# S5's outputs by pairs of octets, and b's gates as two units of seven block products behind w_proj_b

## The chip, the cores and the metric

One core of a Trainium2 chip runs the whole kernel as one launch. The metric is the device time of one execution in microseconds (us), taken as the median over runs. Five engines work side by side, each through its own queue in order: TensorE (PE) multiplies, VectorE (DVE) and ScalarE (ACT) work on elements, GpSimd (POOL) does small things and starts DMAs that add onto their target, and SyncE (SP) starts the plain DMAs.

## The reference, cut to what matters

One encoder layer over 512 tokens of width 1024, in float32. Two mixers run side by side on the normed input n and are merged by gates:

```python
n = rms_norm(h, mix_norm_g[i])
proj = n @ w_in[i]
xa, zu, zv = proj[..., :OFF_U], proj[..., OFF_U:OFF_V], proj[..., OFF_V:OFF_GA]
gate_a = jax.nn.sigmoid(proj[..., OFF_GA:OFF_GB])
gate_b = jax.nn.sigmoid(proj[..., OFF_GB:])
ya = s5_branch(xa, ...)   # two scans, gelu, then y * sigmoid(y @ w_glu)
yb = sgu_branch(zu, zv, ...)
merged = gate_a * (ya @ w_proj_a[i]) + gate_b * (yb @ w_proj_b[i])
h = h + merged @ w_out[i]
h = h + memory_cross_attention(...)
h = h + swiglu(rms_norm(h, ffn_norm_g[i]), w_gate[i], w_up[i], w_down[i])
```

The change touches gate_b, `yb @ w_proj_b` and the end of s5_branch. Each is 1024 wide, but for S5, which is 512 wide: 32 groups of 16 channels with 64 complex states a group.

## The kernel before

**Precision.** Every matrix product takes float32 operands split into a high half (ACT casts, line 85) and a low half (DVE subtracts, line 86) by `split`, and sums three matmuls: high x high, high x low, low x high.

**Weights.** `plan` is a list of weight blocks in the order in which the products use them. `next_w` hands out the next one; on the way it starts the loads of later blocks (each load has its own lead, 3 entries in most cases) and splits blocks up to two entries ahead. Raw blocks, high halves and low halves have three buffers each, so a block can be split when the product three before it is done. `plan_feat` plans blocks of 512 rows and 256 columns. `plan_sums` hangs other transfers on plan entries: sums of blocks of w_q and w_down that are built in DRAM (a plain copy on SP, and some entries later an addition on POOL), for use much later.

**Products.** `feat` computes two groups of 128 output features over all 512 tokens: 2 x 4 x 3 matmuls of 512 columns for a block. `product` (line 1370) is used further on, for the queries and the feed-forward part: there a matrix product is split in 2 x 2 blocks, and seven block products of 256 columns, with sums of blocks taken before and after, stand for eight. The numbers 1 to 7 name them. In the feed-forward units GpSimd and DVE build the sums of the weight blocks (lines 175 to 184).

**Order.** After the projection zu (`zu_evac`, lines 1144 to 1145) makes yb_hi and yb_lo in the slots E and D, the gates of b and w_proj_b alternate by column groups of 256: sigmoid on ACT into `part` (slot A, line 1155), then `pb_evac` multiplies `part` by w_proj_b's result on DVE (line 1158). Then come w_glu and w_proj_a. A scheduler at compile time orders the instructions of each engine, by program order among those that are ready; what is marked `in_order` keeps its order.

**S5 beside it.** `s5_program` is a generator that `tick` advances while the projections run, one unit of `side["now"]` for each 5.2 us of products; `later` calls a function some units on. For each octet of groups `s5_kernels` builds small kernels (through DRAM, kd to tt) and `s5_outputs` makes the outputs: the states are copied, shifted by one (`ss`, lines 952 and 953), `mix_` multiplies (line 966), gelu on ACT (line 972), four transposes (line 978), a copy, and eight stores into `yd` in DRAM, half of them from SP and half from ACT (line 986). The octets go 0, kernels 2, 1, kernels 3, 2, 3. Behind w_proj_b `finish_side` runs out what is left, S5's pool is closed, and a pool "merge" opens; `ygt` is loaded from yd (line 1174), split into yg, and read by w_glu.

**Tags.** Tiles of one tag share buffers: a new tile waits until all uses of the old one are done. `zh` holds S5's states, `u` its inputs, `e0`, `e1`, `tt`, `wt` and `etmp` its work tiles.

Of the kernel before, what the change touches and what calls it, by code (L numbers as in the profile page):

```python
# [9 lines left out]
F32 = mybir.dt.float32  # L10
# [7 lines left out]
P = 128  # L18
D = 1024
# [33 lines left out]
def hybrid_layer_kernel(  # L53
# [157 lines left out]
    def plan_queries():  # L211

        for q, n in ((1, 0), (5, 0), (2, 0), (6, 0), (1, 1), (7, 0), (2, 1), (4, 0), (3, 0),
# [7 lines left out]
            plan.append(((w_q, 512 * n, q), [(LOADS, load)], lambda got=got: halves(got.pop("raw"))))  # L221

    def plan_units(units, down):
# [86 lines left out]
    for i in range(4):  # L310
# [225 lines left out]
    s5 = ExitStack()  # L536
    s5p = s5.enter_context(tc.tile_pool(name="s5", bufs=1))


# [61 lines left out]
    ud = dp.tile([SW, Q, NCH], F32, name="ud")  # L601
    yd = [dp.tile([GO * C, Q, NCH], F32, name=f"yd{o}") for o in range(NO)]
    st = {}
# [25 lines left out]
    def s5_setup():  # L629
# [22 lines left out]
        raw_b = s5p.tile([P, 2, G, C], F32, tag="tt", name="raw_b", bufs=2)  # L652
        raw_c = s5p.tile([P, 2, G, C], F32, name="raw_c")
        brow = s5p.tile([2 * G, 2, 64, C], F32, tag="u", name="brow")
# [92 lines left out]
        yield 1.5  # L747
        zr = s5p.tile([P, G, C], F32, name="bbr")
        zi = s5p.tile([P, G, C], F32, name="bbi")
        w = s5p.tile([P, 2, G, C], F32, tag="etmp", name="bbw")  # L750
# [15 lines left out]
        for j in range(4):  # L766
            nc.sync.dma_start(dcol[32 * j:32 * j + C, :],
                                s5_d[0].rearrange("(q j c) -> j c q", j=4, c=C)[j])
        st["dmask"], st["dcol"] = dmask, dcol
        yield 0.3  # L770
# [170 lines left out]

    def s5_outputs(o):
        gs = slice(o * GO, (o + 1) * GO)
        while ("oct", o) not in st:
            yield None
        e_re, e_im, tt = st["oct", o]
        zh, u = st["zh"], st["u"]
        ss = s5p.tile([P, 2, GO, NCH], F32, tag="wt", name="ss", bufs=2)
        zv = zh[:, :, :, gs].rearrange("p n i g -> p i g n")
        nc.gpsimd.memset(ss[lo_, :, :, 0:1], 0.0)  # L950
        nc.gpsimd.memset(ss[hi_, :, :, NCH - 1:NCH], 0.0)
        nc.scalar.copy(ss[lo_, :, :, 1:NCH], zv[lo_, :, :, 0:NCH - 1])
        nc.scalar.copy(ss[hi_, :, :, 0:NCH - 1], zv[hi_, :, :, 0:NCH - 1][:, :, :, ::-1])
        ss = (ss[:, 0], ss[:, 1])

        yt = tt.rearrange("p (i r) c -> p i r c", i=2)

        def mix_():
            ps = aux("py", (P, GO // 2, P))
            for r in range(GO // 2):  # L960
                for k in range(3):
                    for j in range(2):
                        g = 2 * r + j
                        a = (u[:, o * GO + g, :], ss[0][:, g, :], ss[1][:, g, :])[k]
                        b = (tt[:, g, :], lc(e_re, g), lc(e_im, g))[k]
                        in_order(nc.tensor.matmul(ps[64 * j:64 * j + 64, r, :], a, b, start=r == k == 0, stop=k == 2,  # L966
                                                  tile_position=(0, 64 * j), skip_group_check=True))
            later(0.5, lambda: squash(ps))

        def squash(ps):  # L970

            nc.scalar.activation(yt[:, 0], ps, AF.Gelu_apprx_tanh)
            later(1, back)

        def back():
            ps = aux("pyt", (P, GO // 2, P))
            for r in range(GO // 2):
                nc.tensor.transpose(ps[:, r, :], yt[:, 0, r, :], ident)
            later(0.5, lambda: emit(ps))

        def emit(ps):
            nc.scalar.copy(yt[:, 1], ps)
            y = yt[:, 1].rearrange("p r (g n) -> p (r g) n", n=NCH)
            ydo = yd[o].rearrange("(g c) l n -> l c g n", c=C)
            for l in range(Q):
                (nc.sync, nc.scalar)[l % 2].dma_start(ydo[l], y[C * l:C * l + C])

        later(0.5, mix_)
        yield 0.1
        yield None  # L990

    def s5_program():
# [15 lines left out]
        for _ in range(2):  # L1008
            yield None
        for o in range(NO):  # L1010
            yield from s5_outputs(o)
            if o + 2 < NO:
                yield from s5_kernels(o + 2)

# [138 lines left out]

    def gb_evac(m, j, ps):
        nc.scalar.activation(part[:, m - OFF_GB // P, :], ps, AF.Sigmoid)

    def pb_evac(m, j, ps):
        nc.vector.tensor_tensor(part[:, m, :], ps, part[:, m, :], ALU.mult)

    for c0 in range(0, D, 256):  # L1160
        feat(w_in, OFF_GB + c0, xn, KD, gb_evac)
        feat(w_proj_b, c0, yb, KD, pb_evac)
    finish_side()
    s5.close()
    mgx = ExitStack()
    mgp = mgx.enter_context(tc.tile_pool(name="merge", bufs=1))
    align(mgp)


    yg_hi = mgp.tile([P, 4, T], F32R, name="yg_hi")  # L1170
    yg_lo = mgp.tile([P, 4, T], F32R, name="yg_lo")
    ygt = mgp.tile([P, 4, T], F32, name="ygt")
    for m in range(4):
        nc.sync.dma_start(ygt[:, m, :], yd[m].rearrange("p l n -> p (l n)"))
        split(yg_hi[:, m, :], yg_lo[:, m, :], ygt[:, m, :])
    ya_hi = mgp.tile([P, 4, T], F32R, name="ya_hi")
    ya_lo = mgp.tile([P, 4, T], F32R, name="ya_lo")

    def glu_evac(m, j, ps):
        z = np_.tile([P, T], F32, tag="ev", name="glu", bufs=2)  # L1180
        nc.scalar.activation(z, ps, AF.Sigmoid)
        z2 = np_.tile([P, NCH, Q], F32, tag="ev", name="glu2", bufs=2)
        nc.vector.tensor_tensor(z2.rearrange("p n l -> p l n"), z.rearrange("p (l n) -> p l n", l=Q),
                                ygt[:, m, :].rearrange("p (l n) -> p l n", l=Q), ALU.mult)
        split(ya_hi[:, m, :], ya_lo[:, m, :], z2.rearrange("p n l -> p (n l)"))

    for c0 in range(0, SW, 256):
        feat(w_glu, c0, (yg_hi, yg_lo), 4, glu_evac)

# [4 lines left out]
    for c in range(KD // 2):  # L1194
        gat[c] = mgp.tile([P, 2, T], F32, tag="gat", name="gat", bufs=3)
        nc.sync.dma_start(gat[c], gad[2 * c:2 * c + 2].rearrange("m p t -> p m t"))
# [7 lines left out]
    for c0 in range(0, D, 256):  # L1204
        feat(w_proj_a, c0, (ya_hi, ya_lo), 4, pa_evac)
    mgx.close()

# [76 lines left out]

    K0, K1, T0, T1 = slice(0, 4), slice(4, 8), slice(0, 256), slice(256, 512)
    hops = {q: (hn_hi[:, ks, ts], hn_lo[:, ks, ts])
# [73 lines left out]

    def product(ps, u, q, start, ops):

        hi, lo = next_w(u[0], u[1], q)
        for j in range(2):
            cs = slice(j * P, (j + 1) * P)
            for k in range(4):
                a = (hi[:, k, cs], lo[:, k, cs])
                b = (ops[q][0][:, k, :], ops[q][1][:, k, :])
                for i, (x, y) in enumerate(((0, 0), (0, 1), (1, 0))):
                    nc.tensor.matmul(ps[:, j, :], a[x], b[y], start=start and j == k == i == 0,  # L1370
                                     stop=k == 3 and i == 2, skip_group_check=True)
        tick(2.7)

    def unit_bank(name):
        return bank(name).rearrange("p (j t) -> p j t", j=2)
# [9 lines left out]
    def kept(x, name):  # L1385
        t = np_.tile([P, 2, 256], F32, tag="ev", name=name, bufs=2)
        nc.scalar.copy(t, x)
        return t

    def minus(x, t):  # L1390
        nc.vector.tensor_tensor(t, x, t, ALU.subtract)
        return t


# [380 lines left out]
```

## Time and profile before

| | us |
|---|---|
| runs | 877.23 median of 3 (876.22 to 877.63) |
| the profiled execution | 877.18 |
| its span, first to last instruction | 875.4 |

In the page, busy time is given for each engine as a share of the span; the chain that ended last is the path that is followed back from the last instruction. In the chain in order of time and in a timeline each row has its start, its length, the engine, the line of the kernel and what was written from what. A matmul's row is longer than the distance to the next, as matmuls overlap in the array; the pace is the distance of starts.

### The profile page before, as it was taken

Reading aid. Unit: us, or ns where it says so; the run is one execution under the profiler, and the core shown is the slowest. Engines: PE = TensorE matmul, PEld = TensorE weight load, DVE = VectorE, ACT = ScalarE, POOL = GpSimd, SP = SyncE. Lnnn points to the kernel's source line nnn. Section 1 sums busy time; section 2 is a strip of 40 time slices with the busy share of each in tenths; the row PEclk is TensorE's granted clock in tenths of the full one; section 3 lists DMA queues with packets and bytes.
Section 4 is the critical chain, followed back from the end, with each engine's and each line's share of the span. In section 5 each row is a group of like instructions: output and inputs, shape, how many; then the busy total and the mean of one; then the engine's idle time right before and its main releaser. Section 6 shows DMA issues by size and latency. Waiting matters only on the chain.

```text
span 875.4 us, 14560 instructions
## 1 busy us (share of the span) xinstructions
PE 862.9 (99%) x5753; PEld 759.9 (87%) x5753; DVE 617.4 (71%) x867; ACT 464.1 (53%) x684; POOL 104.9 (12%) x154
## 2 busy tenths in 40 slices
PE   9999999999999999999999999999999999999996
PEld 6787888887888888889899878999999999888875
DVE  5699679968313258669657646767877768898875
ACT  5544875277434234557557444645545454556663
POOL 1001065103311100110000001001111110000000
PEclk9999999999999999999999999999999999999998
DMA  8358369943759946825687144547788963256672
GB/s 260 112 148 249 78 200 257 248 125 107 205 133 278 263 134 211 270 88 174 196 262 218 52 137 128 145 129 187 178 217 212 233 165 79 82 166 198 194 249 87
DMA packets 112134, 154.34 MB, mean 176 GB/s; under 512 B 13545, under 2 KB 78593, under 8 KB 112002
## 3 DMA queue, kind: packets, MB, share of 16 engines
q1 hardware_dynamic: 93042, 128.27, 45.2%
q0 software_dynamic: 16432, 24.09, 16.6%
q10 hardware_dynamic: 2592, 1.05, 0.5%
q8 instruction: 45, 0.74, 0.3%
q14 instruction: 23, 0.19, 0.1%
HBM read 146.60 MB, written 38.24 MB: 211 GB/s over the span
## 4 chain that ended last, share of the span: by engine, by line
PE 93%; DVE 5%; ACT 1%; issue 1%; POOL 0%; POOLq 0%
PE pf L350 29%; PE pt L350 17%; PE px L1370 12%; PE dx L350 7%; PE pq L1370 6%; PE dq L350 3%; PE pv L1370 3%; PE qx L1370 2%; PE dv L350 2%; PE ptr L511 1%; PE py L966 1%; PE po L350 1%; PE qq L1370 1%; DVE wlo L86 1%; PE pz L902 1%; PE pw L883 1%
## 5 line engine op out<-in xcount | busy, mean ns | idle before, releaser
L86 DVE TENSOR_TENSOR wlo<-wraw,whi 128x1024 fp32r<-128x1024 f32 (+1 forms) x139 | 165.0, 1187 | 110.2 <-ACT whi L85 106.9
L85 ACT CAST whi<-wraw 128x1024 fp32r<-128x1024 f32 (+1 forms) x139 | 142.3, 1024 | 168.2 <-PE pf L350 60.1
L350 PE MATMUL pf<-xn,whi 128*128 128x512 f32 x448 | 140.6, 393 | 0.0
L350 PEld LDWEIGHTS pf<-xn,whi 128*128 128x128 f32 x448 | 83.4, 188 | 17.9 <-issue 1.1
L350 PE MATMUL pf<-xn,wlo 128*128 128x512 f32 x224 | 87.7, 391 | 0.0
L1370 PE MATMUL px<-fn,whi 128*128 128x256 f32 x480 | 83.3, 277 | 0.0
L1370 PEld LDWEIGHTS px<-fn,whi 128*128 128x128 f32 x480 | 72.4, 188 | 0.3 <-ACT u L1630 0.2
L85 ACT CAST whi<-b 128x1024 fp32r<-128x1024 f32 x40 | 42.1, 1053 | 50.5 <-PE px L1370 27.1
L86 DVE TENSOR_TENSOR wlo<-b,whi 128x1024 fp32r<-128x1024 f32 x40 | 49.0, 1224 | 28.0 <-ACT whi L85 28.0
L1370 PE MATMUL px<-fn,wlo 128*128 128x256 f32 x240 | 66.5, 277 | 0.0
L350 PE MATMUL dx<-whi,s 128*128 128x512 f32 x170 | 53.9, 392 | 1.4 <-ACT whi L85 1.0
L1370 PE MATMUL pq<-s,whi 128*128 128x256 f32 x320 | 55.1, 277 | 0.0
L86 DVE TENSOR_TENSOR wlo<-t,whi 128x1024 fp32r<-128x1024 f32 x30 | 36.7, 1225 | 20.1 <-ACT whi L85 20.1
L85 ACT CAST whi<-t 128x1024 fp32r<-128x1024 f32 x30 | 31.6, 1052 | 36.0 <-PE pv L1370 12.6
L350 PEld LDWEIGHTS pf<-xn,wlo 128*128 128x128 f32 x224 | 42.1, 188 | 8.6
L1370 PEld LDWEIGHTS pq<-s,whi 128*128 128x128 f32 x320 | 48.3, 188 | 0.1
L1370 PEld LDWEIGHTS px<-fn,wlo 128*128 128x128 f32 x240 | 45.1, 188 | 0.0
L1370 PE MATMUL pq<-s,wlo 128*128 128x256 f32 x160 | 44.3, 277 | 0.0
L350 PE MATMUL pt<-whi,xn 128*128 128x512 f32 x128 | 42.4, 404 | 0.0
L350 PEld LDWEIGHTS dx<-whi,s 128*128 128x128 f32 x170 | 31.7, 188 | 8.4 <-ACT whi L85 1.2
L350 PE MATMUL dx<-wlo,s 128*128 128x512 f32 x85 | 33.1, 390 | 0.0
L1370 PEld LDWEIGHTS pq<-s,wlo 128*128 128x128 f32 x160 | 30.1, 188 | 0.0
(436 smaller groups left out, 2132.1 us busy)
## 6 DMA issues: line engine op xcount, KB each, us to landing
wraw<-in_w_in_dram SPq DMA_DIRECT2D x36, 512.0 KB, 5.2
dsum<-in_w_down_dram SPq DMA_DIRECT2D x20, 512.0 KB, 6.9
wraw<-dsum SPq DMA_DIRECT2D x20, 512.0 KB, 4.1
b<-in_w_gate_dram SPq DMA_DIRECT2D x15, 512.0 KB, 4.1
b<-in_w_up_dram SPq DMA_DIRECT2D x15, 512.0 KB, 3.9
wraw<-in_w_down_dram SPq DMA_DIRECT2D x15, 512.0 KB, 3.8
dsum<-in_w_down_dram POOLq DMA_DIRECT2D x10, 512.0 KB, 7.6
dsum<-dsum POOLq DMA_DIRECT2D x10, 512.0 KB, 7.7
```

The lines of the kernel that those rows point to most:

```text
L85: hi = nc.scalar.copy(dst_hi, src)
L86: lo = nc.vector.tensor_tensor(dst_lo, src, dst_hi.bitcast(F32), ALU.subtract)
L350: nc.tensor.matmul(ps, a[x], b[y], start=start and i == 0, stop=stop and i == 2, skip_group_check=free)
L511: tr = nc.tensor.transpose(ps[:, j, :], src[:, k * P:(k + 1) * P], ident)
L883: nc.tensor.transpose(ps[:, j, :], wt[:, 4 * hf + j, :], ident)
L902: in_order(nc.tensor.matmul(ps[hf, g, :], wt[:, g, hf], x, start=g == 0, stop=True, tile_position=(0, 64 * j), skip_group_check=True))
L966: in_order(nc.tensor.matmul(ps[64 * j:64 * j + 64, r, :], a, b, start=r == k == 0, stop=k == 2, tile_position=(0, 64 * j), skip_group_chec ...
L1370: nc.tensor.matmul(ps[:, j, :], a[x], b[y], start=start and j == k == i == 0, stop=k == 3 and i == 2, skip_group_check=True)
```

## The change

Four things.

1. w_proj_b comes first, all four column groups, and ACT copies its results into `part`.
2. b's gates follow as two units of 512 columns, each of seven block products, in the order `ORDER`. DVE builds sums of blocks of xn (`gate_sum`, `onto`) beside w_proj_b; block 7's operand is overwritten in place, and the sums for 5, 6 and 3 are split into slots D and E, which held yb. The sums of weight blocks are built in a tile `gw` that takes the tag zh. Each finished quarter goes through a sigmoid on ACT and a multiplication into `part` on DVE.
3. S5's outputs go by pairs of octets. The two octets of a pair stand in the two halves of the partitions; gelu writes into a layout in which whole 128 x 128 transposes give w_glu's input, which ACT copies into `ygt` on the chip. yd with its stores and loads is gone. The second pair waits until `side["now"]` is 34. yg is split before the ninth product of the gates.
4. The pool "merge" is gone: its tiles take tags of S5's pool, which closes behind w_proj_a; `gat` takes wt and tt. plan_sums has new places, as the plan is six entries longer and none of them is to lie in entries 30 to 49.

```diff
+    GATES = [(w_in, OFF_GB), (w_in, OFF_GB + 512)]
+    ORDER = ((1, 0), (2, 0), (5, 0), (6, 0), (1, 1), (7, 0), (2, 1), (5, 1), (6, 1), (3, 0), (7, 1), (4, 0), (4, 1), (3, 1))
+    def plan_gates():
...
+            def make(q=q, i=i, b=b, got=got):
+                t, b11 = (gate_place[0](2 * i + j) for j in range(2))
+                if q in (2, 3):
+                    return halves(got.pop("raw"))
+                if q == 5 and i == 0:
+                    nc.vector.tensor_tensor(t, t, got.pop("b12"), ALU.add)
+                ops = halves(b11 if q in (1, 7) else t)
+                if q == 5:
+                    nc.vector.tensor_tensor(t, t, got.pop("raw"), ALU.add)
+                elif q == 6:
+                    nc.vector.tensor_tensor(b11, t, b11, ALU.subtract)
+                    nc.gpsimd.dma_start(t, b(1, 0), accum_op=ALU.add)
+                return ops
+            loads = {1: [(5, whole(2 * i + 1, b(0, 0)))], 2: [(LOADS, plain(b(1, 0)))],
+                     5: [(8, whole(2 * i, b(0, 0))),
+                         (4, plain(b(0, 1), nm="b12")) if i == 0 else
+                         (6, lambda i=i, b=b: nc.gpsimd.dma_start(gate_place[0](2 * i), b(0, 1), accum_op=ALU.add)),
+                         (LOADS, plain(b(1, 1)))],
+                     3: [(LOADS, plain(b(1, 1)))]}
...
     for c0 in range(0, D, 256):
-        plan_feat(w_in, OFF_GB + c0, KD)
         plan_feat(w_proj_b, c0, KD)
+    plan_gates()
...
-    plan_sums([(5 + 3 * i, 3) for i in range(12)] + [(40 + 2 * i, 2) for i in range(8)] +
-              [(79 + 3 * i, 3) for i in range(3)] + [(116 + 5 * i, 4) for i in range(9)])
+    plan_sums([(5 + 3 * i, 3) for i in range(8)] + [(50 + 2 * i, 2) for i in range(7)] +
+              [(85 + 3 * i, 3) for i in range(3)] + [(122 + 5 * i, 4) for i in range(14)])
...
+        yl = octs[0][2].rearrange("p g c -> p (g c)").rearrange("p (l x) -> p l x", l=Q)
         def mix_():
+            both = [aux("py", (P, GO // 2, P)) for i in range(2)]
+            for g in range(GO):
+                ps = both[g // 4][:, g % 4, :]
                 for k in range(3):
+                    for j, (e_re, e_im, tt) in enumerate(octs):
+                        a = (u[:, os_[j] * GO + g, :], states[j][:, 0, g, :], states[j][:, 1, g, :])[k]
                         b = (tt[:, g, :], lc(e_re, g), lc(e_im, g))[k]
+                        in_order(nc.tensor.matmul(ps[64 * j:64 * j + 64, :], a, b, start=g % 4 == k == 0, stop=k == 2,
                                                   tile_position=(0, 64 * j), skip_group_check=True))
...
+        def back(i):
+            ps = aux("pyt", (P, 4, P))
+            for l in range(4):
+                nc.tensor.transpose(ps[:, l, :], yl[:, 4 * i + l, :], ident)
+            later(0.5, lambda: emit(i, ps))
+        def emit(i, ps):
+            y = ygt[p].rearrange("p j (l n) -> p l j n", l=Q)[:, 4 * i:4 * i + 4]
+            nc.scalar.copy(y, ps.rearrange("p l (j n) -> p l j n", j=2))
...
+        yield from s5_outputs(0)
+        for o in range(2, NO):
+            yield from s5_kernels(o)
+        while side["now"] < 34:
+            yield None
+        yield from s5_outputs(1)
...
     def pb_evac(m, j, ps):
-        nc.vector.tensor_tensor(part[:, m, :], ps, part[:, m, :], ALU.mult)
+        nc.scalar.copy(part[:, m, :], ps)
...
+    gops = {1: xq(K0, T0), 2: xq(K1, T0), 7: xq(K0, T1), 4: xq(K1, T1)}
+    def gate_sum(n):
+        if n == 0:
+            gsum[3] = quarter("x3", "etmp")
+            onto(gsum[3], gops[7], ALU.subtract, gops[1])
+        elif n == 1:
+            gsum[1] = quarter("x1", "raw_c")
+            onto(gsum[1], gops[4], ALU.subtract, gops[7])
+            split(*gops[7], gsum[3])
+        elif n == 2:
+            gsum[2] = quarter("x2", "etmp")
+            for i, x in enumerate(gops[1]):
+                V.tensor_tensor(gsum[2], gsum[2 - (i == 0)], x.bitcast(F32), ALU.subtract)
...
+    split(*gops[5], gsum[1])
+    split(*gops[6], gsum[2])
+    onto(gsum[2], gops[2], ALU.add)
+    split(*gops[3], gsum[2])
...
+    def gate_step(q, i):
+        u = GATES[i]
+        if q == 1:
+            gx[i], gv[i] = unit_bank("gx"), unit_bank("gv")
+            product(gx[i], u, 1, True, gops)
+            nc.scalar.copy(gv[i], gx[i])
+        elif q == 2:
+            product(gv[i], u, 2, False, gops)
+            gate_put(i, 0, T0, sigmoid(gv[i]))
+        elif q == 5:
+            gq[i] = unit_bank("gq") if i == 0 else aux("gq").rearrange("p (j t) -> p j t", j=2)
+            product(gq[i], u, 5, True, gops)
+        elif q == 6:
+            product(gx[i], u, 6, False, gops)
+            nc.scalar.copy(u2s[i], gx[i])
+        elif q == 7:
+            product(gx[i], u, 7, False, gops)
+            u3 = minus(gq[i], kept(gx[i], "u3"))
+            gate_put(i, 1, T1, sigmoid(u3, u3))
+        elif q == 4:
+            product(gx[i], u, 4, False, gops)
+            gate_put(i, 0, T1, sigmoid(gx[i]))
+        else:
+            product(gq[i], u, 3, False, gops)
+            u2 = minus(gq[i], u2s[i])
+            gate_put(i, 1, T0, sigmoid(u2, u2))
...
+    for n, (q, i) in enumerate(ORDER):
+        if n == 8:
+            finish_side()
+            yg = [Pieces([s5p.tile([P, 2, T], F32R, tag=tag, name="yg", bufs=2) for c in range(2)])
+                  for tag in ("e0", "e1")]
+            for m in range(4):
+                split(yg[0][:, m, :], yg[1][:, m, :], ygt[m // 2][:, m % 2, :])
+        gate_step(q, i)
```

`gate_put` multiplies a quarter into `part` on DVE, `sigmoid` is one ACT instruction, `kept` an ACT copy, `minus` a DVE subtraction, each over 128 x 512 elements; `onto` is two DVE steps over 128 x 1024, or three with `first`. `product`, `unit_bank`, `kept` and `minus` are moved up from the query part, unchanged.

More of the change, by code (lines that the diff above doesn't have):

```diff
@@ L601, in hybrid_layer_kernel @@
     ud = dp.tile([SW, Q, NCH], F32, name="ud")
-    yd = [dp.tile([GO * C, Q, NCH], F32, name=f"yd{o}") for o in range(NO)]
+    ygt = []
     st = {}
@@ L975, in back @@
[L975 to L986, printed above, removed]
+            later(0.5, lambda: squash(both))
@@ new lines, in squash @@
+        def squash(both):
+            for i, ps in enumerate(both):
+                y = yl[:, :, 64 * i:64 * i + 64].rearrange("p l (g c) -> p g l c", c=C)
+                nc.scalar.activation(y, ps.rearrange("p g (l c) -> p g l c", c=C), AF.Gelu_apprx_tanh)
+            ygt.append(np_.tile([P, 2, T], F32, tag="gain", name="ygt", bufs=2))
+            for i in range(2):
+                later(1 + 0.5 * i, lambda i=i: back(i))
+        def back(i):
[3 more added lines that the diff above has]
+            later(0.5, lambda: emit(i, ps))
@@ L1009, in s5_program @@
             yield None
[L1010 to L1013, printed above, removed]
+        yield from s5_outputs(0)
+        for o in range(2, NO):
+            yield from s5_kernels(o)
+        while side["now"] < 34:
+            yield None
+        yield from s5_outputs(1)
     def finish_side():
@@ L1167, in hybrid_layer_kernel @@
[L1167 to L1177, printed above, removed]
+        nc.scalar.copy(part[:, m, :], ps)
+    K0, K1, T0, T1 = slice(0, 4), slice(4, 8), slice(0, 256), slice(256, 512)
```

158 lines of the change are left out of this document (100 added, 58 removed).

## The prediction

> **What bounds the kernel now.** I read the spans first, then the page's shares and its chain of waits, then busy times by stretch, the chain in order of time, and at last the engines' timelines around the change.
>
> ```profile
> core 0: 875.4 us, clock 0.997
> PE 862.9 (99%) x5753; PEld 759.9 (87%) x5753; DVE 617.4 (71%) x867; ACT 464.1 (53%) x684; POOL 104.9 (12%) x154
> PE 93%; DVE 5%; ACT 1%; issue 1%; POOL 0%; POOLq 0%
> ```
>
> TensorE (PE) is busy for 99% and carries 93% of the chain: time falls when matmul time falls, provided that nothing new makes PE wait. The stretches decide whether there is room for that. After the length, the columns are busy time of PE, weight loads, VectorE (DVE), ScalarE (ACT) and GpSimd, then clock, DMA share and GB/s.
>
> ```profile
> 181.57:340.40 158.83, 158.80 (x958) 130.86 (x958) 77.13 (x89) 75.09 (x89) 29.48 (x53) 1.00 0.65 176
> 280.00:307.40 27.40, 27.40 (x123) 22.69 (x122) 10.03 (x10) 8.08 (x10) 3.10 (x3) 1.00 0.96 277
> 690.00:728.00 38.00, 38.00 (x338) 38.00 (x337) 29.31 (x30) 19.93 (x24) 3.56 (x3) 1.00 0.75 182
> 728.00:766.00 38.00, 36.98 (x296) 35.39 (x295) 31.52 (x32) 21.05 (x25) 0.00 (x0) 1.00 0.22 67
> 766.00:804.00 38.00, 38.00 (x180) 31.95 (x180) 34.88 (x43) 21.90 (x28) 0.00 (x0) 1.00 0.59 181
> ```
>
> From the middle of zu's projection to the end of w_proj_a (first row) PE has no hole, while DVE works 49% and ACT 47%. The third row is two feed-forward units, work of the kind that the gates become: DVE at 77%, PE full. The last has DVE at 92% and PE still full.
>
> **The matmuls.** The chain in order of time (start, length) gives their pace.
>
> ```profile
> 234.18 2.77 PE py L966 x48
> 260.11 80.27 PE pf L350 x354
> 597.79 8.16 PE px L1370 x72
> ```
>
> A 512-column matmul takes 80.27/354 = 0.2267 us, a 256-column one 8.16/72 = 0.1133: the same per column. Before, b's gates are 4 column groups x 2 x 8 x 3 = 192 of 512: 43.52 us. After, they are 14 products of 2 x 4 x 3 = 24 of 256: 14 x 2.72 = 38.08. **Gain 5.44 us.** The Trainium skill speaks against a part of this (TensorE: Matmul & The Clock Gate, Back-to-back issue gap): each matmul of a warm array costs its columns and some 2.5 ns more, so that 336 short ones pay more often than 192 long ones. Its figures, 215.8 and 109.2 ns, would make the gain an estimated 4.7 us; the two rows show no such fixed part, and the rows decide.
>
> **S5's outputs.** mix_ keeps its 24 products for an octet (48 records, 2.77 us) and four transposes for an octet; they come in two blocks instead of four or five.
>
> ```profile
> 180.82 0.39 PE L350 MATMUL pf<-xn,wlo 128*128 128x512 f32 x1
> 181.14 0.44 PE L966 MATMUL py<-tt,u 128*64 128x128 f32 x4
> 181.50 0.73 PE L350 MATMUL pf<-xn,whi 128*128 128x512 f32 x2
> 259.51 0.60 PE L978 MATMUL pyt<-ident,tt 128*128 128x128 f32 x4
> 259.87 0.47 PE L350 MATMUL pf<-yb_hi,whi 128*128 128x512 f32 x1
> 187.61 2.01 ACT L953 COPY ss<-zh 64x1008 f32<-64x1008 f32 x1
> ```
>
> Here pf's pace would have resumed at 181.05; it does at 181.50, 0.45 us for four records worth 4 x 2.77/48 = 0.23. So entering and leaving costs about 0.2, and two or three blocks fewer save 0.4 (between 0 and 0.8). The transposes, 0.36 a group, stay. The 32 stores of yd, the four loads of ygt and their wait go; PE did not wait for them, so I count nothing. The state copies (2.01 us each, four for a pair) were there before.
>
> **Order.** w_proj_b now stands directly behind zu, and reads all of yb.
>
> ```profile
> 216.36 0.59 ACT L1144 ACTIVATE zu<-pf 128x512 f32<-128x512 f32 x1
> 219.47 0.68 DVE L86 TENSOR_TENSOR yb_lo<-zu,yb_hi 128x512 fp32r<-128x512 f32 x1
> ```
>
> The last yb is ready at 220.15, 3.8 us after its activation began. The first block of w_proj_b needs only the first half of yb and takes 24 x 0.2267 = 5.44 us; the last two tiles of yb are wanted 1.4 us later still. Hidden, with 3 us to spare; without that cover it costs up to 3.8.
>
> **What DVE and ACT get.** First groups (count, busy, mean ns, idle before), then four DVE starts and two ACT starts that give the spacing in a queue (in brackets: idle before, and what ended it).
>
> ```profile
> L86 DVE TENSOR_TENSOR wlo<-b,whi 128x1024 fp32r<-128x1024 f32 x40 | 49.0, 1224 | 28.0 <-ACT whi L85 28.0
> L85 ACT CAST whi<-b 128x1024 fp32r<-128x1024 f32 x40 | 42.1, 1053 | 50.5 <-PE px L1370 27.1 <-PE pq L1370 18.0 <-DMA b<-in_w_gate_dram 2.3
> L1155 ACT ACTIVATE part<-pf x8: 590/596/601, 222.2 to 297.6; 128x512 f32<-128x512 f32 x8
> L1158 DVE TENSOR_TENSOR part<-pf,part x8: 683/692/692, 232.9 to 307.8; 128x512 f32<-128x512 f32 x8
> 593.15 1.22 DVE L184 TENSOR_TENSOR b<-t,b 128x1024 f32<-128x1024 f32 x1
> 594.29 1.22 DVE L86 TENSOR_TENSOR wlo<-t,whi 128x1024 fp32r<-128x1024 f32 x1
> 595.43 0.68 DVE L1643 TENSOR_TENSOR u<-pq,u 128x512 f32<-128x512 f32 x1
> 596.04 1.22 DVE L184 TENSOR_TENSOR t<-t,b 128x1024 f32<-128x1024 f32 x1
> 584.11 1.05 ACT L85 CAST whi<-t 128x1024 fp32r<-128x1024 f32 x1 [1.18 <-PE px L1370]
> 585.07 0.58 ACT L1527 COPY pv<-px 128x512 f32<-128x512 f32 x1
> ```
>
> In a queue a 1024-element DVE step takes 1.14 us, a 512 one 0.61, a cast 0.96. Over the whole stretch DVE gets 6 more weight halves, 5 weight sums, 14 steps for the sums of xn (10 of onto and gate_sum, 4 low halves): 25 x 1.22 = 30.5, and 12 evacuations for 8, +2.8. So 77 becomes 110 of some 154 us: room on average. ACT: 10 casts and 14 small steps more, 19 us on 75. But it lies unevenly. gops[5], [6] and [3] are put into slots D and E, which w_proj_b reads to its last matmul. So behind that matmul (t = 0) and within the gates' 38.1 us DVE has 12 weight halves, 4 weight sums, 5 steps for xn, two halves for w_glu (23 x 1.14 = 26.2), 10 evacuations and 4 halves of yg (14 x 0.61 = 8.5): 34.7 us, 91%.
>
> Walking the queues by these spacings: at t = 0.2 to 2.7 ACT does w_proj_b's last copy and the two casts of gops, then the cast for (5,0); the copy gx to gv falls to 3.6, and (2,0), which stands directly behind (1,0) in ORDER and adds onto gv, starts at 4.3 instead of 2.7: **1.6**. (DVE's onto and the sum behind (5,0) come before the half for (6,0), which ends at 10.6; its third matmul wants it at 9.8: **0.9**. gops[3] and the difference for (7,0) put that half to 16.9 against 16.1: **0.9**.) Behind these DVE is level with PE. That makes 3.4 us, less the two groups of transposes of S5's second pair, 0.7, which fall due just there and fill holes: 2.7. The other end is 0, as the 92% row has no hole; but nothing had to start behind a barrier there. I take **2.3**, near the walk.
>
> **DMA and queues.** The gates fetch 14 blocks of 512 KB in place of 8, three of them as additions on GpSimd's queue: 14 x 0.524 = 7.3 MB over some 54 us (three blocks of w_proj_b and the gates), 136 GB/s, against the 277 that 280 to 307 carried without a hole. plan_sums leaves plan entries 30 to 49 free of sums, so on GpSimd the three additions stand behind S5's transfers alone. The sums pushed back land in entries up to 191, the last units and w_down's start, where 728 to 766 shows DMA at 0.22 and GpSimd idle. Nothing counted.
>
> **Sum.** The profiled execution took 877.18 us, its span and 1.78 around it; the median of the runs is 877.23, 0.05 above. 877.23 - 5.44 - 0.4 + 2.3 = **873.7**.
>
> **Rivals.** (a) No new hole: 877.23 - 5.44 - 0.4 = 871.4. For it: the feed-forward units; against it: (2,0) directly behind (1,0), which no unit has. (b) DVE binds all through the gates. The 40 halves of b waited 28.0/40 = 0.7 us each for their cast; 0.4 before each of 14 eats the gain: about 876.9. Against it: those idle times stood where DVE had room. (c) The gates' place is late. It lies in S5's tile zh, which the second pair's state copies must have read. From the point where the side program lets that pair start three blocks remain, 16.3 us; four copies (8.0), a load and a cast follow.
>
> ```profile
> wraw<-in_w_in_dram SPq DMA_DIRECT2D x36, 512.0 KB, 5.2
> t<-in_w_gate_dram POOLq DMA_DIRECT2D x5, 512.0 KB, 7.1
> gat<-gad SPq DMA_DIRECT2D x4, 512.0 KB, 13.9
> 842.00:875.00 33.00, 25.85 (x122) 21.18 (x120) 20.69 (x30) 15.62 (x26) 3.36 (x4) 0.93 0.46 159
> ```
>
> 8.0 + 5.2 + 1.05 = 14.3: hidden by 2 us. With everything 4 us later, PE waits 2 more: about 876. (d) **Slower**: the second unit's addition of b(1,0) onto t by GpSimd. It can start when the difference for (7,1) is done, by the walk at t = 25, and the cast for (4,1) wants it at 33. An addition lands in 7.1; up to 8 it is hidden. Where gat's loads, now free to start early, and w_glu's and w_proj_a's take the queues, 13.9 has been seen: then PE stands for 6 before (4,1), and 873.7 + 6 = 879.7. The Trainium skill (TensorE: Matmul & The Clock Gate, Part 1: The HAM clock gate) adds that an idle window of some 3.4 us halves the clock until a busy one has passed. Here only the tail, where PE idles, has a lower clock (0.93); by that rule (d) would cost an estimated 1.7 more.
>
> **How the numbers follow.** Forecast 0.45, (a) 0.22, (b) 0.10, (c) 0.10, (d) 0.13. The likeliest gives 873.7, by its own bounds (holes of 1 to 3.4) 872.0 to 875.2. The range goes from no hole and 0.8 saved at S5, 871.0 and a little less, up to (b) and a part of (d): 870.7 to 877.6. About 0.2%, 1.75 us, can be told from no change. Faster: nearly all of the forecast, all of (a) and a third of (c): 0.71. Same: (b), the rest of (c), a little of the forecast: 0.14. Slower: (d) and tails: 0.15.
>
> **What would show it.** 336 products at 0.1133 in place of 192 matmuls at 0.2267; PE waiting for ACT at gv and for DVE's halves within 20 us behind w_proj_b, 1 to 3.4 us in all; DVE over 85% busy in the gates; PE full elsewhere. A wait before (1,0) speaks for (c), before (4,1) for (d). I am wrong if the holes lie behind zu, or if the units or w_down get holes from the sums pushed back.

## The result, and the profile after

| | runs | median us | ratio to before (95% interval) |
|---|---|---|---|
| before | 8 | 877.25 | |
| changed | 8 | 874.62 | 0.9972 (0.9962 to 0.9983) |
| changed, in a second session | 5 | 873.51 (before there 877.31) | 0.9951 (0.9939 to 0.9964) |

Faster, by 2.6 us in one session and 3.8 in the other; 873.7 had been predicted. The profiled execution took 875.6 us, its span 873.8. The spans, the page's busy times and its chain:

```profile
core 0: 873.8 us, clock 0.991
PE 860.3 (98%) x5897; PEld 764.8 (88%) x5897; DVE 648.0 (74%) x897; ACT 475.6 (54%) x704; POOL 108.8 (12%) x157
PE 95%; DVE 1%; DMA 1%; SPq 1%; ACT 0%; issue 0%; POOLq 0%; POOL 0%; ACTq 0%
```

TensorE still carries nearly all of the chain. Busy times of the changed kernel by stretch, columns as in the prediction; the first two rows are the changed stretch and b's gates alone:

```profile
183.00:338.30 155.30, 155.28 (x1105) 134.72 (x1104) 108.04 (x118) 86.70 (x109) 27.76 (x50) 1.00 0.61 164
265.40:305.80 40.40, 40.40 (x345) 40.40 (x345) 31.39 (x34) 26.18 (x37) 3.86 (x3) 1.00 0.72 194
728.00:766.00 38.00, 36.98 (x287) 35.01 (x286) 31.49 (x31) 20.73 (x24) 1.63 (x2) 1.00 0.51 131
```

DVE's busy time is 108 of 155 us where it was 77 of 159, and PE has no hole in the gates. The last row shows what the moved weight sums do: GpSimd works where it was idle, and the DMA share is 0.51 instead of 0.22.

Where the time went is read from the chain in order of time (start, length, work, matmuls). Before, with S5's products and the two ends of the stretch:

```profile
152.29 7.14 PE psv L1131 x64
...
181.21 0.37 PE py L966 x4
...
192.69 2.55 PE py L966 x44
...
207.75 2.84 PE py L966 x48
...
251.69 2.77 PE py L966 x48
...
340.38 4.76 PE pt L350 x21
```

After, the same, with the beginning and the end of b's gates. psv and pt are the matmuls of the sgu branch ahead of the change and of w_out behind it:

```profile
154.00 7.14 PE psv L1185 x64
...
182.92 0.37 PE py L1015 x4
...
194.40 0.36 PE py L1015 x2
...
196.59 5.17 PE py L1015 x90
...
248.49 0.36 PE py L1015 x2
...
259.96 0.11 PE gx L1221
260.08 5.38 PE py L1015 x94
265.46 2.94 PE gx L1221 x23
268.40 0.87 PE pyt L1032 x8
269.27 2.74 PE gq L1221 x24
272.01 2.86 PE gv L1221 x24
...
291.93 2.49 PE gq L1221 x22
294.42 8.62 PE gx L1221 x72
...
305.78 32.66 PE pf L393 x144
...
338.44 6.57 PE pt L393 x29
```

From psv to pt the stretch took 340.38 - 152.29 = 188.09 us and takes 338.44 - 154.00 = 184.44: **3.65 less**. The fourteen products take the time from 259.96 to 305.78 less S5's two rows in it (py 5.38, pyt 0.87), 39.57 us, where 192 matmuls took 43.52: 3.95 less. S5's products (py) went from 11.30 to 11.64 (the row of 234.18 in the prediction belongs to the first sum). That makes 3.6; the rest is unchanged within 0.1. What follows, from the first matmul of w_out to the end, took 535.2 us before and takes 535.5 (the tail in the table below).

The start differs more: psv begins 1.7 us later in this execution. Before psv PE has the same 1,024 matmuls in both kernels, and in the second profiled execution of the changed kernel psv stood at 152.81, 1.2 us earlier. What moves the start was not found. So the execution that was first profiled shows less gain (1.6 us of span) than the medians do.

Two things in these rows weren't foreseen. S5's second pair, 94 products in 5.38 us, stands exactly between w_proj_b's end (259.96) and the gates; and product 5 (gq) goes ahead of product 2 (gv), as the scheduler may choose among the products that are ready. And 22 products on the sums of xn take 2.49 us, 113 ns each, while 72 on xn itself take 8.62, 120 ns each.

### The profile page after: what moved, and what is told of

The parts are those of the page before. It is cut to its first block, busy times and chain, and to the rows that moved or that the text cites. A ratio compares the mean times of both kernels' runs of the same rounds, so it can differ in the third digit from the quotient of the medians.

```text
span 873.8 us, 14852 instructions
## 1 busy us (share of the span) xinstructions
PE 860.3 (98%) x5897; PEld 764.8 (88%) x5897; DVE 648.0 (74%) x897; ACT 475.6 (54%) x704; POOL 108.8 (12%) x157
## 4 chain that ended last, share of the span: by engine, by line
PE 95%; DVE 1%; DMA 1%; SPq 1%; ACT 0%; issue 0%; POOLq 0%; POOL 0%; ACTq 0%
PE pf L393 27%; PE pt L393 18%; PE px L1221 12%; PE dx L393 7%; PE pq L1221 6%; PE dq L393 3%; PE pv L1221 3%; PE gx L1221 3%; PE qx L1221 2%; PE dv L393 2%; PE py L1015 1%; DMA slab<-in_s_log_step_dram 1%; PE gq L1221 1%; PE ptr L554 1%; PE po L393 1%; PE qq L1221 1%
## 5 line engine op out<-in xcount | busy, mean ns | idle before, releaser
L86 DVE TENSOR_TENSOR wlo<-wraw,whi 128x1024 fp32r<-128x1024 f32 (+1 forms) x135 | 160.0, 1185 | 82.4 <-ACT whi L85 82.0
L85 ACT CAST whi<-wraw 128x1024 fp32r<-128x1024 f32 (+1 forms) x135 | 138.0, 1023 | 145.0 <-PE pf L393 46.9
L393 PE MATMUL pf<-xn,whi 128*128 128x512 f32 x320 | 100.4, 393 | 0.0
L393 PEld LDWEIGHTS pf<-xn,whi 128*128 128x128 f32 x320 | 59.5, 188 | 12.7 <-issue 0.7
L393 PE MATMUL pf<-xn,wlo 128*128 128x512 f32 x160 | 62.6, 392 | 0.0
L393 PE MATMUL pt<-whi,xn 128*128 128x512 f32 x128 | 45.4, 430 | 1.9 <-ACT xn L85 1.9
L393 PEld LDWEIGHTS pf<-xn,wlo 128*128 128x128 f32 x160 | 30.1, 188 | 6.3 <-issue 0.2
L311 POOL DMA_DIRECT2D dsum<-in_w_down_dram x12 | 13.3, 1108 | 163.3 <-DMA dsum<-in_w_down_dram 163.3
```

The costliest lines, as they stand in the source:

```text
L85: hi = nc.scalar.copy(dst_hi, src)
L86: lo = nc.vector.tensor_tensor(dst_lo, src, dst_hi.bitcast(F32), ALU.subtract)
L311: plan[j + step][1].append((0, lambda d=dst, x=more: nc.gpsimd.dma_start(d, x, accum_op=ALU.add)))
L393: nc.tensor.matmul(ps, a[x], b[y], start=start and i == 0, stop=stop and i == 2, skip_group_check=free)
```

## The experiments

All kernels are the changed one with one edit (two in one case); each ratio is to before on the same chip. "Stretch" is the distance of starts from the first psv to the first matmul of w_out, "tail" what follows, both in the profiled execution.

| kernel | median us | ratio (95% interval) | stretch | tail |
|---|---|---|---|---|
| before | 877.25 | | 188.1 | 535.2 |
| changed | 874.62 | 0.9972 (0.9962, 0.9983) | 184.4 | 535.5 |
| changed, again | 873.51 | 0.9951 (0.9939, 0.9964) | 184.3 | 535.6 |
| gates_plain | 878.37 | 1.0014 (0.9999, 1.0028) | 188.5 | 537.8 |
| no_cover | 876.55 | 0.9982 (0.9970, 0.9995) | 186.7 | 537.1 |
| close_korder | 876.17 | 0.9985 (0.9976, 0.9995) | 186.6 | 536.0 |
| xn_apart | 877.12 | 0.9996 (0.9983, 1.0008) | 185.6 | 535.4 |
| sums_flat | 877.09, one run | | 185.3 | 538.7 |
| xn_by_64 | 875.49 | 0.9976 (0.9965, 0.9987) | 184.8 | 536.0 |
| xn_by_128 | 876.39 | 0.9984 (0.9972, 0.9997) | 185.4 | 536.2 |
| xn_lo_by_256 | 875.47 | 0.9971 (0.9959, 0.9983) | 184.3 | 538.6 |
| start_in_order | 877.99 | 1.0006 (0.9993, 1.0018) | 188.8 | 536.8 |
| sums_close | 873.89 | 0.9958 (0.9942, 0.9974) | 184.5 | 535.8 |
| sums_close, again | 873.92 | 0.9954 (0.9935, 0.9972) | 184.3 | 535.7 |

**Is the gain the block products'?** gates_plain keeps w_proj_b ahead, S5 by pairs and everything else, and computes b's gates as four column groups of 512-column matmuls.

```diff
-    plan_gates()
+    for c0 in range(0, D, 256):
+        plan_feat(w_in, OFF_GB + c0, KD)
...
+    def gb_evac(m, j, ps):
+        z = np_.tile([P, T], F32, tag="ev", name="gs", bufs=2)
+        nc.scalar.activation(z, ps, AF.Sigmoid)
+        nc.vector.tensor_tensor(part[:, m - OFF_GB // P, :], part[:, m - OFF_GB // P, :], z, ALU.mult)
...
-        gate_step(q, i)
+        feat(w_in, OFF_GB + c0, xn, KD, gb_evac)
```

> One part alone: S5 by pairs and w_proj_b first are kept, b's gates are computed as before, by four column groups of eight blocks of 512 columns, each with a sigmoid and a multiplication into part; the sums of xn and of weight blocks are left out, and the places of the other sums are moved six entries forward. Theory E (all of the gain is the gates' 14 products, 39.7 us for 43.5): PE needs 3.9 us more than in the changed kernel, 878.5, or 1 us over the kernel before. Theory F (S5's new layout and the order bring part of the gain): between 875.5 and 877.2.

The stretch is 188.5 us, 0.4 more than before, and S5's products take 11.64 us there too. So all of the gain is in the fourteen products, and order and S5's pairs by themselves give nothing: in this profile they cost 0.4.

**What hides the work behind w_proj_b?** no_cover ties the matmuls of w_proj_b's last group to their place in the program, so that S5's second pair goes ahead of them and no longer stands between w_proj_b and the gates.

```diff
+            if pin_pe[0]:
+                in_order(ins)
...
+        pin_pe[0] = n == 3
```

> The matmuls of w_proj_b's last column group keep program order, so that the products of S5's second pair stand ahead of that group and not between w_proj_b and the gates. Theory C (my walk was right about the queues, and the pair's 5.2 us of PE work hid the barrier): with the cover gone PE waits 1 to 3.4 us in the first 12 us of the gates, and the time is 875.6 to 878. Theory D (the order in which the scheduler puts product 5 ahead of product 2 is enough, and DVE has room): waits below 0.5 us in all, time as the changed kernel's, 874.6.

First DVE's timeline in the changed kernel, from the point where w_proj_b ends, then PE and DVE in no_cover (in brackets: idle before, and what ended it):

```profile
260.85 1.23 DVE L86 TENSOR_TENSOR gsd<-x,gsd 128x1024 fp32r<-128x1024 f32 x1 [4.20 <-ACT gsd L85]
...
270.13 1.22 DVE L86 TENSOR_TENSOR wlo<-gw,whi 128x1024 fp32r<-128x1024 f32 x1
```

```profile
263.97 0.48 PE L1224 MATMUL gx<-xn,whi 128*128 128x256 f32 x2
...
275.20 0.39 PE L1224 MATMUL gx<-gse,wlo 128*128 128x256 f32 x1 [1.51 <-DVE wlo L86]
```

```profile
264.66 1.23 DVE L86 TENSOR_TENSOR gsd<-x,gsd 128x1024 fp32r<-128x1024 f32 x1 [4.21 <-ACT gsd L85]
...
270.45 0.69 DVE L86 TENSOR_TENSOR yg<-ygt,yg 128x512 fp32r<-128x512 f32 x1
...
272.19 0.69 DVE L86 TENSOR_TENSOR yg<-ygt,yg 128x512 fp32r<-128x512 f32 x1
...
273.93 3.50 DVE L86 TENSOR_TENSOR wlo<-gw,whi 128x1024 fp32r<-128x1024 f32 x3
```

The barrier is the end of w_proj_b, as the slots D and E are free only then. In the changed kernel DVE does the first half behind it at 260.85, 4.6 us ahead of the gates' own first block (265.46). The low half of product 6's weights is the tenth step of DVE's queue from there; it is done at 271.35 and wanted at 274.95, 3.6 us later. In no_cover the queue starts at 264.66, 0.7 us behind the first product's start, and the tenth step (the first of the three in the last row) at 273.93: PE stands 1.51 us before that product's third matmul, the place where the prediction had put its second wait. Two of the ten steps are halves of yg, S5's output, which the pair has made by then. The other waits that the prediction named did not show. The stretch grew by 2.2 us, of which 1.5 are this wait and 0.8 a wait of `pk`, the products that build S5's small kernels, for GpSimd. The medians alone don't separate no_cover from the changed kernel's first session: the intervals overlap.

close_korder showed the same by accident. It was to combine closer places of the last weight sums (below) with another order of S5's products, k = 1, 2, 0, so that a pair's block need not stop for its states.

```diff
-              [(85 + 3 * i, 3) for i in range(3)] + [(122 + 5 * i, 4) for i in range(14)])
+              [(85 + 3 * i, 3) for i in range(3)] + [(122 + 3 * i, 3) for i in range(14)])
...
-                for k in range(3):
+                for n_, k in enumerate((1, 2, 0)):
```

> Two edits on the changed kernel: the last fourteen weight sums every third entry (as sums_close), and S5's products over k in the order 1, 2, 0, so that a pair's block isn't split by a wait for the state's part. Theory H (the sums) gives 0.7 less than the changed kernel on the same chip, and the S5 part another 0.3 to 0.6 (the blocks of py, which took 0.4 us more than before the change although they are fewer, enter once less each): 1.0 to 1.3 below after_again, ratio to before 0.9955 to 0.9962. Rival P (the gain of sums_close was chance, and the entries of py cost the same whatever k comes first): ratio 0.997 as after_again.

Neither theory held: it is slower than the changed kernel by 0.0034 of before's time in one session. Its chain:

```profile
218.39 0.12 POOL gw L261
218.50 1.22 issue
219.73 0.58 POOL bd L840 x2
...
220.78 0.43 PE pk L864 x8
...
248.09 0.80 PE py L1015 x10
...
258.42 4.95 PE py L1015 x86
263.37 1.62 PE pf L393 x6
```

```profile
276.63 0.38 PE L1221 MATMUL gx<-gse,wlo 128*128 128x256 f32 x1 [1.60 <-DVE wlo L86]
```

The second pair takes 0.80 + 4.95 = 5.75 us, against 0.36 + 5.38 = 5.74: nothing saved. But the block is ready a little sooner and so lies ahead of w_proj_b's last six matmuls. The cover is gone, product 6's half is again the tenth step behind the barrier, with two of yg ahead of it, and the wait of 1.6 us before product 6 is back. The first rows are the other wait: GpSimd's addition onto gw waits for its target, S5's small kernel tile bd stands behind it in the queue, and PE's pk waits for bd.

**The pace of the products.** By the first theory the pace hangs on the distance in SBUF from the weights to the moving operand (the one that streams past them), modulo 256 bytes. By the places that the compiler gives the tiles it is 0 for the halves of xn and 192 for the sums of xn; the offset `APART` that the query part uses should make all products go every 113 ns. xn_apart gives it to xn, sums_flat takes it from the sums.

```diff
-    xn_hi, xn_lo = token_slot("xn")
+    xn_hi, xn_lo = token_slot("xn", APART)
```

> xn is laid with its halves shifted by 48 and 112 elements, as hn and fn are. In the changed kernel the gates' 256-column matmuls start every 0.120 us where the moving operand is xn, and every 0.1133 where it is gsd or gse; 192 read xn. Theory A (the place of the moving operand in SBUF sets the pace): the 192 go to 0.1133 too, 192 x 0.0067 = 1.3 us less on PE in the gates, the median about 873.3; the 512-column matmuls on xn stay at 0.227. Theory B (xn is slow because its blocks are cut out of rows of 512, or because DVE and ACT read it at that time): 0.120 stays, and the time too, 874.6.

```diff
-    gops[5], gops[6] = halves_at(gd, 4, 256, APART), halves_at(ge, 4, 256, APART)
-    gops[3] = (at_(gd, 2176 + APART[0]), at_(ge, 2048 + APART[1]))
+    gops[5], gops[6] = halves_at(gd, 4, 256, (0, 0)), halves_at(ge, 4, 256, (0, 0))
+    gops[3] = (at_(gd, 2048), at_(ge, 2048))
```

> The other way round: the sums of xn for block products 5, 6 and 3 are laid without the shift of 48 and 112 elements. Theory A (place): their 144 matmuls go from 0.1133 to 0.120 us, 1.0 us more in the gates. Theory B (cut rows, or readers beside it): they stay at 0.1133.

sums_flat did as expected: all its products go every 120 ns, those on the sums too, and the gates take 0.9 us more. xn_apart did not. Lengths of 276, 281 and 283 ns go with distances of starts of 113, 118 and 120; groups of the changed kernel, then of xn_apart (shortest/median/longest, first and last start):

```profile
L1221 PE MATMUL gx<-xn,wlo x48: 278/283/283, 265.6 to 302.8; 128*128 128x256 f32 x48
L1221 PE MATMUL gx<-gse,wlo x16: 276/276/279, 274.9 to 291.7; 128*128 128x256 f32 x16
```

```profile
L1221 PE MATMUL gx<-xn,wlo x48: 276/281/281, 265.0 to 302.2; 128*128 128x256 f32 x48
L1221 PE MATMUL gx<-gse,wlo x16: 281/281/281, 274.3 to 291.1; 128*128 128x256 f32 x16
```

Products on xn gained 2 ns, and those on the sums, which the edit doesn't touch, lost 5: all go every 118 ns. Beside that the 480 matmuls of 512 columns on xn go every 233 ns instead of 227 in the median, 237.8 instead of 232.0 in the mean: 2.8 us lost. Three more places were tried.

```diff
+    xn_hi, xn_lo = token_slot("xn", (16, 16))   # xn_by_64
+    xn_hi, xn_lo = token_slot("xn", (32, 32))   # xn_by_128
+    xn_hi, xn_lo = token_slot("xn", (0, 64))    # xn_lo_by_256
```

> Both halves of xn are moved by 16 numbers (64 bytes) in SBUF; nothing else differs. Theory L (the matmuls' pace hangs on where the moving operand lies against the weights, by 256 bytes: at distance 0 the 512-column ones start every 227 ns and the 256-column ones every 120, at distance 192 every 233 and every 113 to 118, as the rows of the two kernels so far show): at distance 64 one of the two paces changes. If both are the good ones (227 and 113), the 192 gate matmuls on xn save 192 x 6.7 ns = 1.3 us and the time is 873.3; if the 512-column ones go to 233 as at 192, the some 480 pf matmuls and the time lose 2 to 3 us, 877. Rival M (only the two halves' distance from each other, or the history of the stream, sets the pace): gates at 120 and 512 columns at 227 as before, 874.6.

> Both halves of xn are moved by 32 numbers (128 bytes) in SBUF; nothing else differs. Theory L (the pace hangs on the distance by 256 bytes): at distance 128 the paces are new ones: 227 and 113 give 873.3, 233 and 113 to 118 about 877, 227 and 120 leave 874.6. Rival M (only the distance of the two halves from each other or the history of the stream matters): 227 and 120, 874.6.

> Only the low half of xn is moved, by 64 numbers (256 bytes), so that both halves keep their distance 0 to the weights by 256 bytes and differ from each other by 256 of 512 bytes, as the operands with the pace 113 do; nothing else differs. Theory N (two conditions: 512-column matmuls are fast where the distance to the weights is 0 by 256 bytes, 256-column ones where the two halves of the moving operand lie in different halves of 512 bytes): 512 columns stay at 227, the 192 gate matmuls on xn go from 120 to 113, and the gates take 1.3 us less: 873.3. Rival L (only the distance to the weights matters): 227 and 120, 874.6. Rival O (the pace of a stretch is also a state that it falls into at its first product): the gates at 118 throughout, as with xn moved by 64 bytes, 874.6 to 875.

Median paces of the 512-column matmuls on xn, the gate products on xn and those on the sums: 227, 120 and 113 ns in the changed kernel; 229, 118 and 118 by 64 bytes; 232, about 120 and 114 by 128, where the products on xn vary from 115 to 122; 233, 118 and 118 by 192 (xn_apart); 227, 120 and 113 with the low half alone moved by 256. The distance to the weights by 256 bytes matters and the halves' distance from each other does not (theory N falls), but no place gave both good paces, and the sums of xn, which stay in place when xn is moved, go at 113 in one kernel and at 118 in another. Nothing was gained.

**The start.** Was the late psv of the first profile a wait of ACT, whose first exponential of S5 waits for a table, with xn's casts behind it?

```diff
-        A_.activation(stp, ls, AF.Exp)
+        in_order(A_.activation(stp, ls, AF.Exp))
```

> ScalarE's first exponential of S5, which waits for a small table from DRAM, is tied to its place in the program, so that the casts of xn stand ahead of it; nothing else differs. Theory J (the 1.7 us by which the profile of the changed kernel was late at its first psv matmul are this one wait of ScalarE, the casts standing behind a transfer): psv starts at 150.5 to 152.0 us and the time falls by 0.5 to 1.7 us, to 873 to 874. Rival K (the start is bound by the loads of x and of the weights, whatever ScalarE does first): psv starts at 151.5 to 154 as in the other runs and the time is 874.2 to 875.

psv starts at 150.6 us, the earliest of all, and the time is 3.4 us above the changed kernel's in the first session: neither theory as a whole. PE's timeline in psv:

```profile
152.76 0.71 PE L1185 MATMUL psv<-wsx,zt 128*128 128x128 f32 x4 [1.32 <-ACT zt L1124]
...
159.70 2.05 PE L1185 MATMUL psv<-wsx,zt 128*128 128x128 f32 x16 [0.57 <-DVE sv L1186]
```

psv takes 10.9 us now instead of 7.1, as its operands and banks come late from ACT and DVE; behind it pk waits for bd (0.4), and the gates, S5's rows in them left out, take 0.3 us more. What is won ahead of psv is lost in it.

This run also bears on what hides the work behind w_proj_b. With S5 late, the second pair comes 17 us behind w_proj_b's end (260.3), inside the gates. Nothing covers the barrier here but two products of 0.36 us, and yet PE has no wait in the gates. The pair in the chain, then DVE's first step behind the barrier, product 6's low half, and the matmul that wants it:

```profile
277.85 5.38 PE py L1015 x94
```

```profile
261.38 1.22 DVE L86 TENSOR_TENSOR gsd<-x,gsd 128x1024 fp32r<-128x1024 f32 x1 [0.56 <-ACT gsd L85]
...
268.31 1.22 DVE L86 TENSOR_TENSOR wlo<-gw,whi 128x1024 fp32r<-128x1024 f32 x1
...
269.83 0.28 PE L1221 MATMUL gx<-gse,wlo 128*128 128x256 f32 x1
```

The half is the seventh step of DVE's queue, not the tenth: yg can't be split yet, as the pair isn't done, and the second step of `onto` comes behind the half. It is done at 269.53, 0.3 us before PE wants it. So the missing cover alone doesn't make the wait; it takes DVE's queue in the order of no_cover as well.

**The sums pushed back.** In the changed kernel the last fourteen weight sums lie in plan entries 122 to 191, and GpSimd adds until the end of w_down's first part. sums_close sets them every third entry (122 to 164); it was run in two sessions.

```diff
-              [(85 + 3 * i, 3) for i in range(3)] + [(122 + 5 * i, 4) for i in range(14)])
+              [(85 + 3 * i, 3) for i in range(3)] + [(122 + 3 * i, 3) for i in range(14)])
```

> The last fourteen weight sums stand every third entry of the plan (122 to 161) instead of every fifth (122 to 187); nothing else differs. Theory H (the sums that were pushed back cost time at the end: their transfers and GpSimd's additions run at 740 to 806 us, beside w_down's own weights, and in some executions w_down's halves come late): GpSimd is idle from 766 to 806 as before the change, no matmul of w_down waits for a half, the tail from the first w_out matmul to the end is about 535.2 us in the profile, and the median falls by 0.4 to 1.0 from 874.6, to 873.6 to 874.2 (the holes of 1 to 2.5 us that sums_flat, no_cover and gates_plain showed there would be in a part of the executions of the changed kernel too). Rival I (the holes there come from something else, or denser sums only move the collision into the units): the time is 874.4 or more, with waits for a half at 560 to 740 us or the same ones after 780.

> The kernel of sums_close once more: the last fourteen weight sums every third entry of the plan; nothing else differs from the changed kernel. The changed kernel has been measured at ratios of 0.9972 and 0.9951 to before, sums_close at 0.9958. Theory H (the sums' overlap with w_down costs the changed kernel 0.5 us or more on the mean): the ratio is 0.9955 or less, and the profile has no wait of w_down for a half of a weight between 780 and 806 us. Rival I (what the holes in w_down cost is within what differs from session to session): the ratio lies between 0.9955 and 0.9975, whether the profile has such waits or not.

Stretches of the second run of sums_close (its GpSimd and DMA), then waits in w_down's first part in xn_lo_by_256, whose sums stand as in the changed kernel:

```profile
740.00:766.00 26.00, 24.98 (x180) 23.01 (x179) 22.80 (x23) 14.53 (x16) 0.00 (x0) 1.00 0.25 75
786.00:806.00 20.00, 20.00 (x90) 16.58 (x89) 17.79 (x22) 12.64 (x17) 0.00 (x0) 1.00 0.63 197
```

```profile
789.38 0.50 PE L393 MATMUL dv<-wlo,s 128*128 128x512 f32 x1 [0.53 <-DVE wlo L86]
797.91 0.73 PE L393 MATMUL dv<-whi,s 128*128 128x512 f32 x2 [0.24 <-ACT whi L85]
```

With the sums early, GpSimd is idle there and the DMA share from 740 to 766 us is 0.25, near the 0.20 of before the change and not the 0.49 of the changed kernel. Of the ten profiles with the sums late, five have such waits between 780 and 806 us (sums_flat, no_cover, gates_plain, start_in_order and xn_lo_by_256), with tails of 536.8 to 538.7; the other five have none, the changed kernel's own two among them, with tails of 535.4 to 536.2. Of the three profiles with the sums early none has one. That fits theory H, but none of three beside five of ten can be chance. In time this can't be told apart: 0.9958 and 0.9954, between the changed kernel's 0.9972 and 0.9951. The waits are shown; that the late sums cause them, and that taking them away is worth anything for the median, is not, though neither session speaks against it. No version was found that beats the changed kernel beyond what is measured.

## Why the prediction came out right

The time was right, and the sum close: the prediction's terms give -5.44 - 0.4 + 2.3 = -3.5, and the stretch came out at -3.65. But that was luck. Three of its terms were off, by +1.5, +0.8 and -2.3, and they cancelled. Of the signs that the prediction named for its forecast, three did not come: 144 products go at 0.1133 and not 336, PE does not wait behind w_proj_b, and DVE is busy for 78% of the gates and not over 85%.

- **The block products: -5.44 predicted, -3.95 measured.** The count was right (336 matmuls), the pace only for 144 of them. The step that failed is "a 256-column one 0.1133: the same per column", a row of the feed-forward units carried over to operands in another place. The 192 on xn itself go at 0.120: 192 x 0.0067 = 1.3 us. gates_plain shows that this term is the whole gain, sums_flat that the place of the operand bears on the pace, and xn_apart that the place alone doesn't set it. The estimate of 4.7 by the Trainium skill (TensorE: Matmul & The Clock Gate, Back-to-back issue gap) came nearer, but not for its reason, a fixed cost of each matmul: those on the sums go at half the pace of 512 columns to the nanosecond, and the loss sits in the other operand. By the rule all 336 would have paid; the trace doesn't agree. The section gives this formula for an isolated matmul, not for a stream as here.
- **S5 in fewer blocks: -0.4 predicted, +0.4 measured.** The number of blocks was counted from the code. The scheduler lets the first two or four products go as soon as they are ready and the rest later, so there are still five, and the products take 11.64 us, not 11.30. Another order of k saved nothing.
- **Holes behind w_proj_b: +2.3 predicted, 0 measured.** The walk started DVE's and ACT's queues with the gates at t = 0 and took both queues and products in the order of the program. Two things came out otherwise. S5's second pair, 5.4 us, stands between w_proj_b and the gates; I had counted 0.7 us of the pair, its transposes, and taken its products as due earlier. And the scheduler chooses the order. Where both the cover is gone and ten steps of DVE stand ahead (no_cover, close_korder), a wait of 1.5 to 1.6 us appears at one of the three places that the walk named, product 6's third matmul, where it had put 0.9. Where the cover is gone but the half is the seventh step (start_in_order), there is no wait. The waits that the walk put at gv and at (7,0) stand in no profile. That product 5 ahead of product 2 takes away the one at gv fits no_cover, where ACT's copy to gv ends at 267.98 while PE does product 5 from 267.27, but it was not tested apart.
- **yb behind zu: hidden, as predicted.** No hole stands there in any profile.
- **The rivals.** (a), no new hole, is what the trace shows, but its time, 871.4, needed the gain of 5.44. (b) fell: DVE is busy 31.39 of 40.40 us in the gates, 78%. The work had been counted rightly, 34.7 us behind w_proj_b and 35.9 measured from 259.96 to 305.78, but with the pair there it had 45.8 us to spread over and not 38.1: hence 78% and not the 91% of the walk. (c) and (d) fell: no wait before (1,0) or (4,1).
- **DMA and queues: counted at nothing, and not quite nothing.** w_down waits in half of the profiles with the sums late, as the last lines of the prediction had named as a way to be wrong: 0.2 to 0.6 us each, and a tail longer by 1 to 3 us than the changed kernel's. And in close_korder GpSimd's addition onto gw, which was to stand behind S5's transfers alone, holds up bd; pk waits 0.4 to 0.8 for bd in no_cover and start_in_order too.

What stays open: why the changed kernel's two sessions differ by 0.002, what moves the start by 1 to 2 us, and how much of the 535 us behind the change moves with the sums.

## What to carry to other kernels

Before counting a queue's work behind a barrier, ask two things: what the scheduler can put on the bounding engine just there, and in which order it will put the queue itself. Here 5 us of other products hid a queue of ten steps, and an edit elsewhere that let these products start a little sooner brought 1.6 us of waiting back; with three of the steps behind the one that PE waits for, nothing had to be hidden. Take a pace from rows with the same operand in the same place, not from the same shape. When many terms are summed, a right total doesn't show that they are right: compare the terms.

## What the runs showed of the hardware

The same matmul of 128 x 128 by 256 columns mostly goes at one of three steady paces, 113, 118 or 120 ns (only with xn moved by 128 bytes do the starts vary, from 115 to 122), and one of 512 columns at 227 to 233. Where the moving operand lies against the weights, modulo 256 bytes, plays a part: at distance 0, 512 columns go at 227 and 256 columns at 120; at 192 bytes, 233 and 113 or 118. It isn't the whole: the sums of xn, at the same place in both, go at 113 in the changed kernel and at 118 in xn_apart, and in the chain of the changed kernel products that bear the same names, at the same distance, go at 118 and then at 113.

```profile
573.78 2.83 PE pq L1221 x24
...
590.46 5.44 PE pq L1221 x48
```

That is 117.9 and 113.3 ns, with a granted clock of 1.00. A stretch seems to keep the pace that it fell into; what sets it wasn't found.
